# Stages ahead of attention in a one-layer hybrid trunk: six raw weight tiles for four, 36- and 64-row transposes on all 128 rows, another order of the first products and of what stands between them

## The chip, the cores and the metric

One core of a Trainium2 chip runs the kernel. The metric is the device time of one execution in microseconds. All rows named "profile" come from one execution taken by the hardware profiler.

## The reference, cut to what matters

One layer (DEPTH is 1) on 512 tokens of 1024 channels, all in fp32: a norm, one wide projection, a pooling mixer and a sparse-attention mixer side by side, a gated merge, and an MLP.

```python
h = rms_norm(x, norm_mix[l])
proj = h @ w_in[l]
u, q, kc, vc, ksl, vsl, kwn, vwn, g_nsa, g_merge = jnp.split(proj, IN_SPLITS, axis=-1)
y_pool = pool_mixer(u, w_pool[l], pool_scale[l])
y_nsa = nsa_mixer(q, kc, vc, ksl, vsl, kwn, vwn, g_nsa, pe_k[l], pe_v[l],
                  w_ck1[l], w_ck2[l], w_cv1[l], w_cv2[l]).astype(x.dtype)
merged = g_a * (y_pool @ w_proj_pool[l]) + g_b * (y_nsa @ w_proj_nsa[l])
x = x + merged @ w_out[l]
h = rms_norm(x, norm_mlp[l])
x = x + jnp.square(jax.nn.relu(h @ w_ff1[l])) @ w_ff2[l]
```

Inside the attention mixer, blocks of 32 keys and of 32 values are compressed by a small MLP each, which is what most of the stages ahead of attention prepare:

```python
flat = blocks.transpose(0, 1, 3, 2, 4).reshape(B, n_cmp, G, CMP_LEN * dh)
return jax.nn.gelu(flat @ w1) @ w2
```

## The kernel before, in words

**Products in three parts.** A product of fp32 operands is made from split operands: a high part (rounded to the type float32r) and a low part (what is left). Three matmuls follow for each chunk of 128 channels: high by high, low weights by high tokens, high weights by low tokens. In the rows, `wh` and `wl` are the high and low parts of a weight tile; `R_64` and `R_65` (both `R` in the profile) are the high and low parts of the normed, transposed tokens; `wkt` holds both parts of a compression weight.

**Weights.** A weight comes as a raw tile of up to 128 x 1024 fp32 (512 KB) by a DMA that is issued from SyncE's queue (`emit_load`, L297). Raw tiles are taken in turn from a ring of RAW = 4 buffers, so a load waits until the tile four loads earlier has been converted. `emit_prep_half` converts a tile in two halves: the high part by ScalarE (L524; POOL L522 in the very first), the low part by a subtraction on VectorE or, for the first two weights, on POOL (both L527). `ahead()` issues the next piece of this preparation; it is called between groups of products.

**The start.** The four token tiles x0 to x3 are loaded. For each, `sums0` takes the sum of squares (ScalarE L793, L794) and scales the tile (VectorE L796, L799); `turn0` transposes it on TensorE, eight blocks of 128 x 128 (L807); `evac0` takes the blocks out of PSUM into the high part (ScalarE L815) and the low part (VectorE L817). For tiles 2 and 3 `evac0` also copies the blocks to a buffer MA (ScalarE L820), which the gates of the merge use much later. `token_sums` adds high and low parts of the tokens into MA, two such sums early on (VectorE L1142). `fm_halves` (L700) makes the first two products, the compression keys `ck` and the selection keys `ks`, in halves of 256 tokens: first both keys on tiles 0 and 1, then both on tiles 2 and 3. Between them a side generator, `others()`, is stepped: it emits the transposes and evacuations of tiles 2 and 3, after every twelfth product.

**Up to attention.** A list written by hand, P1, sets the order: ck, ks, u0, wk0, u1, wk1, u2, wk2, kw, wk3, cv, V0, V1, V2, wv0, u3, wv1, q0, wv2, the pool products, wv3, gates, the other queries. `cmp_first` takes ck (or cv) from PSUM to a scratch tile with the tokens of each block beside each other (ScalarE L963, L966), adds the position rows (VectorE L973) and splits the result into the operand cA (VectorE L976, L979). `cmp_mlp1` multiplies it by the compression weights wk0 to wk3 or wv0 to wv3 (TensorE L997, eight products of 256 columns each). `cmp_rest` applies the activation, transposes two blocks of 64 rows (L1022), takes them out with a scale (ScalarE L1025) and makes the second compression product (L1035 for keys, L1050 for values). The pooling mixer works on the u tiles (VectorE L1083 to L1095, TensorE psF<-yd,wpl). `rope` turns keys and queries with help of a small DMA `rs<-rx` from SyncE (L882) that exchanges halves.

**From attention on.** Attention takes some 180 to 365 us of the span, the merge and output projection follow, and the MLP runs to the end. Sums of several weight products are prepared in DRAM by accumulating DMAs that POOL issues (L343), in attention too, where POOL also scales the attention rows P (L1423).

TensorE's instructions run in the order in which the program issues them, which a scheduler sets; `behind(x)` (an issue_after) only says that an instruction is placed after x.

Of the kernel before, what the change touches and what calls it, by code (L numbers as in the profile page):

```python
# [62 lines left out]
def trunk(ctx: ExitStack, tc: tile.TileContext, A, out):  # L63
    nc = tc.nc
# [37 lines left out]
    WL, LD = [], []  # L102
    RAW = 4

# [166 lines left out]
    raws, hls = {}, {}  # L271
    st = {"load": 0, "prep": 0, "use": 0, "kept": 0, "pairs": 0, "sums": 0}
    spare, slots_hl = [], []
# [4 lines left out]
    def emit_load():  # L278

        i = st["load"]  # L280
        if i >= len(LD):
            return False
        segs = LD[i]
        a = segs[0][0].shape[1]
        b = sum(s.shape[2] for s, _ in segs)
        assert a * b <= 1024
        if not by_name() or st["kept"] < RAW:
            st["kept"] += by_name()
            t = wp.tile([128, 1024], F32, tag="raw", bufs=RAW, name=f"raw{i}")
        elif spare:  # L290
            t = spare.pop(0)
        else:
            return False
        st["load"] += 1
        v = t[:, :a * b].rearrange("p (a b) -> p a b", a=a)
        for s, o in segs:
            began[0] = nc.sync.dma_start(v[:, :, o:o + s.shape[2]], s)  # L297
        raws[i] = (t, a, b)
        for _ in range(sums_after(i)):
            make_sum(began[0])  # L300
        while i in EARLY[1:] and begun:
            add_sum()
        if (26 <= i < N1 and len(begun) > 1) or i >= N1 + len(FILL2) + 4 and (len(begun) > 2 or begun and st["sums"] == len(jobs)):
            add_sum()
        while i == MLP0 + 6 and len(begun) > 2:
            add_sum()
        return True
# [379 lines left out]
    def fm_halves(keys, psp, posts, tag, xT):  # L687

        ws, ps = [], []
        for h in range(2):  # L690
            tok = slice(256 * h, 256 * h + 256)
            for i, k in enumerate(keys):
                if h == 0:
                    ws.append(use(k))
                    ps.append(psp.tile([128, S], F32, tag=tag[0], bufs=tag[1], name="psF"))
                prods = fm_products(ws[i][0], ws[i][1], xT, tok=tok)
                if h == 0:
                    prods = prods[0::3] + prods[2 - i::3] + prods[1 + i::3]
                for j, (a, b) in enumerate(prods):
                    last_mm[0] = PE.matmul(ps[i][:, tok], a, b, start=h == 0 and j == 0,  # L700
                                           stop=h == 1 and j == len(prods) - 1, skip_group_check=True)
                    if j % 12 == 11:
                        ahead()
                        step_side()
                if h == 1:
                    r = posts[i](ps[i])
                    if r is not None:
                        side.append(r)
                yield
# [31 lines left out]
    PC = ap.tile([128, NT, 2, 64], FR, name="PC")  # L741
    rows = early_f[1][0:36, 0:128]
    w2 = {kv: f[:, 1824:1952].rearrange("p (k c) -> p k c", k=2) for kv, f in zip("vk", early_f)}
# [10 lines left out]
    for h in range(2):  # L754
        for r in (slice(0, 96), slice(96, 127)):
            DVE.memset(grow[r, 512 * h:512 * h + 512], 0.0)
    ACT.dma_start(xt[0], x_d[0:128, :])
    nc.sync.dma_start(xt[1], x_d[128:256, :])
# [27 lines left out]
    def behind(made):  # L786
        return tc.issue_after(made.ins)
# [13 lines left out]

    def turn0(i):
        trs[i] = []
        for a in range(2):
            pt = ps1.tile([128, 4, 128], F32, tag="V", bufs=4, name="psTr")
            for k in range(4):
                PE.transpose(pt[:, k, :], xt[i][:, 512 * a + 128 * k:512 * a + 128 * k + 128], ident)  # L807
            trs[i].append(pt)

    def evac0(i, after=None, root=None):  # L810
        sl = slice(128 * i, 128 * i + 128)
        for a in range(2):
# [3 lines left out]
            with behind(after) if after else nullcontext():  # L816
                v = DVE.tensor_tensor(hT[1][:, ks, sl], trs[i][a], hT[0][:, ks, sl].bitcast(F32), op=ALU.subtract)  # L817
        for a in range(2 if i > 1 else 0):
            c = 128 * (i - 2)
            ACT.activation(quarter(MAf, 2 * a + 1)[:, :, c:c + 128], trs[i][a], AF.Copy)  # L820
        return r, v
# [8 lines left out]
    with behind(r):  # L830
        r, scaled2 = sums0(2)
    mode["first"] = ACT
# [3 lines left out]
    with behind(conv[0]):  # L836
        root3, v = sums0(3)
    mode["first"] = None
# [3 lines left out]
    def others():  # L842

        yield
        for i in (2, 3):
            with behind(last_mm[0]):
                turn0(i)
            made[:] = evac0(i, v, root3)
            yield

# [7 lines left out]
    c0.close()  # L858
    made0 = list(made)
    with behind(made[0]):  # L860
        ACT.activation(tick, rr[3][:, 1:2], AF.Sigmoid)
# [78 lines left out]
    with ExitStack() as c1:  # L940
# [64 lines left out]
        def cmp_rest(kv, ps):  # L1005
            t = early_f[0][0:64, 1056:1824].rearrange("p (a n) -> p a n", a=3)
            z, b, c = t[:, 0], t[:, 1], t[:, 2]
            ACT.activation(b, ps[64:128, :], AF.Copy)
# [9 lines left out]
            for _ in range(14 if kv == "v" else 9):  # L1018
                yield
            pt = ps1.tile([128, 2, 64], F32, tag="M", bufs=2, name="psM")  # L1020
            for i in range(2):
                PE.transpose(pt[:, i, :], b[:, 128 * i:128 * i + 128], ident[0:64, 0:64])  # L1022
            gt = p1.tile([128, 2, 64], F32, tag="cg", bufs=2, name="cg")
            with tc.high_priority(60):
# [7 lines left out]
            if kv == "k":  # L1032
                for e in range(2):
                    for i in range(2):
                        PE.matmul(pm[:, e, :], w2d[:, i, e, :], gt[:, i, :], start=i == 0, stop=i == 1,  # L1035
                                  skip_group_check=True)
# [11 lines left out]
            else:  # L1048
                for i in range(2):
                    PE.matmul(pm[0:64, 0, :], gt[:, i, :], w2["v"][:, i, :], start=i == 0, stop=i == 1,  # L1050
                              skip_group_check=True)
                yield
                for g in range(2):
                    for o in range(2):
# [5 lines left out]
                                           op0=ALU.mult, op1=ALU.mult)  # L1060

        wpl = [p1.tile([128, 4, 128], FR, name=f"wpl{e}") for e in range(2)]
        dest["wpool"] = [w.rearrange("p g c -> p (g c)") for w in wpl] + ["wpool"]
# [70 lines left out]
        def token_sums():  # L1134
# [5 lines left out]
            for b in ("11", "21"):  # L1140
                with behind(made0[1] if b == "21" else scaled2):
                    DVE.tensor_tensor(xq[b], *(v.bitcast(F32) for v in parts[b]), op=ALU.add)  # L1142
                yield
                yield
# [44 lines left out]
        first_posts += [lambda ps: list(cmp_first("k")(ps)).clear(), lambda ps: rope(ps, -0.125, k_done(0))]  # L1189
        pr = ps1.tile([128, 36], F32, tag="M", bufs=2, name="psM")  # L1190
        PE.transpose(pr, rows, ident[0:36, 0:36])
        DVE.tensor_copy(pec, pr)
        for _ in first:
# [891 lines left out]
```

## Time and profile before

| what | value |
|---|---|
| median of 3 runs | 770.54 us (770.27 to 772.26) |
| span of the profiled execution | 767.4 us |
| what lies around the span, median less span | 3.1 us |
| TensorE busy | 756.7 us (99%) |
| VectorE busy | 666.4 us (87%) |
| ScalarE busy | 511.1 us (67%) |
| POOL busy | 184.2 us (24%) |
| granted TensorE clock | full speed in every slice |

The page gives no time of its own for the profiled execution, only its span; the median of the runs is 3.1 us longer. In the timeline a row is a group of instructions of one kind: its start, its busy time, engine, line, operation, output and inputs, and in brackets how long the engine was idle ahead of it and what it waited for. Matmuls overlap, and their ends are modelled, so a group's cost is best read from its start to the start of the next group.

### The profile page before, as it was taken

Reading aid. Unit: us, or ns where it says so; the run is one execution under the profiler, and the core shown is the slowest. Engines: PE = TensorE matmul, PEld = TensorE weight load, DVE = VectorE, ACT = ScalarE, POOL = GpSimd, SP = SyncE. Lnnn points to the kernel's source line nnn. Section 1 sums busy time; section 2 is a strip of 40 time slices with the busy share of each in tenths; the row PEclk is TensorE's granted clock in tenths of the full one; section 3 lists DMA queues with packets and bytes.
Section 4 is the critical chain, followed back from the end, with each engine's and each line's share of the span. In section 5 each row is a group of like instructions: output and inputs, shape, how many; then the busy total and the mean of one; then the engine's idle time right before and its main releaser. Section 6 shows DMA issues by size and latency. Waiting matters only on the chain.

```text
span 767.4 us, 13409 instructions
## 1 busy us (share of the span) xinstructions
PE 756.7 (99%) x4757; PEld 675.9 (88%) x4757; DVE 666.4 (87%) x1279; ACT 511.1 (67%) x977; POOL 184.2 (24%) x264
## 2 busy tenths in 40 slices
PE   9999999999999999999999999999999999999996
PEld 7889889888888888888889899989998999889985
DVE  7897999548988889989689689997989788978897
ACT  7766655328878888898745576954774477447754
POOL 4001010117746766574000200111111110111001
PEclk9999999999999999999999999999999999999999
DMA  9559993983051833371357965989998999799942
GB/s 308 165 143 266 251 230 108 257 214 115 15 176 52 158 56 70 56 138 60 116 186 220 324 111 185 287 219 299 310 259 222 314 303 257 215 325 294 293 171 110
DMA packets 119886, 150.76 MB, mean 196 GB/s; under 512 B 5782, under 2 KB 92346, under 8 KB 119611
## 3 DMA queue, kind: packets, MB, share of 16 engines
q1 hardware_dynamic: 98250, 122.90, 48.3%
q0 software_dynamic: 21280, 26.22, 22.8%
q8 instruction: 38, 0.62, 0.3%
q10 hardware_dynamic: 288, 0.79, 0.3%
q14 instruction: 30, 0.24, 0.1%
HBM read 145.16 MB, written 54.53 MB: 260 GB/s over the span
## 4 chain that ended last, share of the span: by engine, by line
PE 84%; DVE 9%; ACT 2%; DMA 2%; issue 1%; POOL 1%; SPq 0%; DVEq 0%; ACTq 0%; POOLq 0%
PE psB L638 20%; PE psB L1698 18%; PE psF L568 16%; PE psB L568 6%; PE psV L638 5%; PE psS L1378 4%; PE psT L1440 4%; PE psO L1474 4%; PE psB L1647 3%; DMA raw<-w_in 2%; PE psF L700 1%; DVE wl L527 1%; DVE PT L1456 1%; DVE P L1400 1%; DVE wkt L527 1%
## 5 line engine op out<-in xcount | busy, mean ns | idle before, releaser
L343 POOL DMA_DIRECT2D S<-w_ff x44 | 49.0, 1113 | 351.3 <-DMA S<-w_ff 290.3
L568 PE MATMUL psF<-R,wh 128*128 128x512 f32 x384 | 124.6, 400 | 0.0
L390 ACT ACTIVATE wh<-raw 128x1024 fp32r<-128x1024 f32 x73 | 77.1, 1058 | 70.0 <-PE psB L638 24.0
L1423 POOL TENSOR_SCALAR P<-P,sm,GT 128x128 f32<-128x128 f32 (+3 forms) x128 | 85.5, 724 | 68.8 <-DVE sm L1420 36.1
L395 DVE TENSOR_TENSOR wl<-raw,wh 128x1024 fp32r<-128x1024 f32 x73 | 88.9, 1219 | 12.7 <-ACT wh L390 12.2
L568 PEld LDWEIGHTS psF<-R,wh 128*128 128x128 f32 x384 | 68.8, 188 | 11.4 <-issue 0.2
L1410 ACT ACTIVATE P<-P,sm 128x128 f32<-128x128 f32 (+3 forms) x128 | 71.0, 557 | 9.9 <-DVE sm L1400 6.2
L568 PE MATMUL psF<-R,wl 128*128 128x512 f32 x192 | 75.5, 393 | 0.0
L524 ACT ACTIVATE wh<-raw 128x512 fp32r<-128x512 f32 (+1 forms) x76 | 45.1, 616 | 32.9 <-PE psF L568 21.2
L1400 DVE CUSTOM_DVE_ANT_0 P<-psS,cst 128x128 f32<-128x128 f32 (+3 forms) x128 | 59.3, 482 | 4.9 <-PE psT L1440 2.7
L390 ACT ACTIVATE w3h<-raw 128x1024 fp32r<-128x1024 f32 x37 | 39.2, 1059 | 34.0 <-PE psB L638 12.6
L527 DVE TENSOR_TENSOR wl<-raw,wh 128x512 fp32r<-128x512 f32 (+1 forms) x74 | 51.5, 707 | 9.2 <-ACT wh L524 8.9
L1451 ACT ACTIVATE PT<-psT 128x512 fp32r<-128x512 f32 (+2 forms) x96 | 49.0, 520 | 13.9 <-PE psT L1440 13.0
L1456 DVE TENSOR_TENSOR PT<-psT,PT 128x512 fp32r<-128x512 f32 (+2 forms) x96 | 56.2, 591 | 1.5 <-ACT PT L1451 1.3
L1440 PE MATMUL psT<-ident,P 128*128 128x128 f32 x320 | 50.1, 273 | 0.6 <-POOL rx L899 0.4
L395 DVE TENSOR_TENSOR w3l<-raw,w3h 128x1024 fp32r<-128x1024 f32 x37 | 45.1, 1220 | 4.7 <-ACT w3h L390 4.5
L1474 PE MATMUL psO<-PT,VV 128*128 128x256 f32 x320 | 48.5, 286 | 0.0
L1440 PEld LDWEIGHTS psT<-ident,P 128*128 128x128 f32 x320 | 39.6, 140 | 9.4 <-POOL rx L899 0.8
L638 PE MATMUL psB<-R,wh 128*128 128x256 f32 x336 | 46.3, 279 | 0.0
L1474 PEld LDWEIGHTS psO<-PT,VV 128*128 128x128 f32 x320 | 42.2, 188 | 1.3 <-ACT PT L1451 0.3
L638 PEld LDWEIGHTS psB<-R,wh 128*128 128x128 f32 x336 | 42.5, 188 | 0.2
L568 PEld LDWEIGHTS psF<-R,wl 128*128 128x128 f32 x192 | 36.0, 188 | 7.5
(442 smaller groups left out, 2083.7 us busy)
## 6 DMA issues: line engine op xcount, KB each, us to landing
raw<-w_ff SPq DMA_DIRECT2D x54, 512.0 KB, 6.2
S<-w_ff POOLq DMA_DIRECT2D x44, 512.0 KB, 8.2
raw<-S SPq DMA_DIRECT2D x44, 512.0 KB, 5.3
S<-w_ff SPq DMA_DIRECT2D x32, 512.0 KB, 7.3
raw<-w_in SPq DMA_DIRECT2D x31, 512.0 KB, 4.7
S<-S SPq DMA_DIRECT2D x12, 512.0 KB, 6.7
raw<-w_proj_nsa SPq DMA_DIRECT2D x8, 512.0 KB, 4.1
x<-x SPq DMA_DIRECT2D x7, 512.0 KB, 6.5
```

Of the source, the lines that this page charges most:

```text
L390: ACT.activation(h, t, AF.Copy)
L395: DVE.tensor_tensor(l, t, h.bitcast(F32), op=ALU.subtract)
L527: eng.tensor_tensor(l[:, sl], t[:, sl], h[:, sl].bitcast(F32), op=ALU.subtract)
L568: PE.matmul(ps, a, b, start=first and j == 0, stop=last and j == n - 1, skip_group_check=True)
L638: PE.matmul(out, w[u][:, k, 128 * f:128 * f + 128], moving[v][:, k, :], **kw)
L1400: DVE.tensor_tensor_reduce(out=P[:, o:o + n].rearrange("p (a c) -> p a c", c=128), in0=s, in1=m, scale=1.0, scalar=3e38, op0=ALU.add, op1= ...
L1410: last_exp[:] = [ACT.activation(c, c, AF.Exp, bias=sm[:, 0, e:e + 1], scale=-1.0, accum_out=sm[:, 1, e:e + 1])]
L1423: r = POOL.tensor_scalar(P[:, o:o + n], P[:, o:o + n], sm[:, 2, e:e + 1], GT[:, qb, c + e:c + e + 1], op0=ALU.mult, op1=ALU.mult)
L1440: PE.transpose(pt[:, 128 * j:128 * j + 128], P[:, 128 * j:128 * j + 128], ident)
L1456: return DVE.tensor_tensor(dL, src, dH.bitcast(F32), op=ALU.subtract)
L1474: PE.matmul(ps[:, qb % 2, :, :], VV[:, k, b, g, :], t[:, j, :, :], start=False, stop=last and j == len(kbs) - 1 and t is tL, skip_group_ch ...
L1698: PE.matmul(ps[f], self.Y.of(y)[u][:, 2 * g + k, 128 * f:128 * f + 128], w[v][:, k, :], start=first and g == k == u == v == 0, stop=g == k ...
```

## The change

1. **Six raw tiles.** RAW goes from 4 to 6. Each raw tile takes 4 KB of every partition; the 8 KB come from the scratch space for the descriptors of POOL's DMAs, which goes from the default of 16384 to 8192 bytes. Two loads more are issued behind the first products, and at load N1 (where attention's loads begin) two calls of `emit_load` do nothing, so that from there on the loads are again four tiles ahead until the MLP.
2. **First products.** In the first half, ck goes high by high, low tokens, low weights (before: low weights second). ks keeps its order.
3. **Tiles 2 and 3.** Their transposes come one half (four blocks) at a time, after products 30, 32, 40 and 44 of the 48, for all eight blocks of a tile in two steps.
4. **Copies and sums.** The four copies to MA come after the last evacuation, and the first token sum comes there too, before behind the scaling of tile 2.
5. **Padding.** The transpose of the 36 rows of positions and scales works on 128 rows (one more memset of 128 x 128 on VectorE at the start), the two transposes in `cmp_rest` work on 128 rows in place of 64 (one more memset of 64 x 256 on POOL), with an output of 128 x 256; L1050's product goes to all 128 rows. The buffer `cg` goes from two copies to one.

```diff
-    RAW = 4
+    RAW = 6
...
+        if i == N1 and st["spared"] < 2:
+            st["spared"] += 1
+            return True
...
                 if h == 0:
-                    prods = prods[0::3] + prods[2 - i::3] + prods[1 + i::3]
+                    prods = prods[0::3] + prods[1::3] + prods[2::3]
...
                     if j % 12 == 11:
                         ahead()
+                    if j % 12 == 11 if h else 24 * i + j + 1 in (30, 32, 40, 44):
                         step_side()
...
-    rows = early_f[1][0:36, 0:128]
+    rows = early_f[1][:, 0:128]
...
+    DVE.memset(rows, 0.0)
...
-        for a in range(2 if i > 1 else 0):
-            c = 128 * (i - 2)
-            ACT.activation(quarter(MAf, 2 * a + 1)[:, :, c:c + 128], trs[i][a], AF.Copy)
...
     def others():
-        yield
         for i in (2, 3):
-            with behind(last_mm[0]):
-                turn0(i)
-            made[:] = evac0(i, v, root3)
-            yield
+            for a in range(2):
+                with behind(last_mm[0]):
+                    turn0(i, (a,))
+                if a:
+                    made[:] = evac0(i, scaled3, root3)
+                yield
+        for i in (2, 3):
+            for a in range(2):
+                c = 128 * (i - 2)
+                with behind(made[0]):
+                    ACT.activation(quarter(MAf, 2 * a + 1)[:, :, c:c + 128], trs[i][a], AF.Copy)
...
+    with behind(made[0]):
+        for _ in range(2):
+            emit_load()
...
-            t = early_f[0][0:64, 1056:1824].rearrange("p (a n) -> p a n", a=3)
-            z, b, c = t[:, 0], t[:, 1], t[:, 2]
+            t = early_f[0][:, 1056:1824].rearrange("p (a n) -> p a n", a=3)
+            turn = t[:, 1]
+            z, b, c = (t[0:64, i] for i in range(3))
...
-            pt = ps1.tile([128, 2, 64], F32, tag="M", bufs=2, name="psM")
+            pt = ps1.tile([128, 2, 128], F32, tag="M", bufs=2, name="psM")
             for i in range(2):
-                PE.transpose(pt[:, i, :], b[:, 128 * i:128 * i + 128], ident[0:64, 0:64])
-            gt = p1.tile([128, 2, 64], F32, tag="cg", bufs=2, name="cg")
+                PE.transpose(pt[:, i, :], turn[:, 128 * i:128 * i + 128], ident)
+            gt = p1.tile([128, 2, 128], F32, tag="cg", bufs=1, name="cg")
...
-                    PE.matmul(pm[0:64, 0, :], gt[:, i, :], w2["v"][:, i, :], start=i == 0, stop=i == 1,
+                    PE.matmul(pm[:, 0, :], gt[:, i, :], w2["v"][:, i, :], start=i == 0, stop=i == 1,
...
+        POOL.memset(early_f[0][64:128, 1312:1568], 0.0)
...
-                with behind(made0[1] if b == "21" else scaled2):
+                with behind(made0[1]):
                     DVE.tensor_tensor(xq[b], *(v.bitcast(F32) for v in parts[b]), op=ALU.add)
...
-        PE.transpose(pr, rows, ident[0:36, 0:36])
-        DVE.tensor_copy(pec, pr)
+        PE.transpose(pr, rows, ident)
+        DVE.tensor_copy(pec, pr[:, 0:36])
...
-    nc = bacc.Bacc("TRN2", target_bir_lowering=False, num_devices=1)
+    nc = bacc.Bacc("TRN2", target_bir_lowering=False, num_devices=1, dynamic_dma_scratch_size=8192)
```

The order on TensorE, first halves of ck and ks, before (a name's number tells one buffer from another: wh_216 and wl_217 are ck's weight, wh_258 and wl_259 ks's, x_157 and x_158 token tiles 2 and 3):

```order
L700 MATMUL psF<-R_64,wh_216 128x256 x8
L700 MATMUL psF<-R_64,wl_217 128x256 x8
L700 MATMUL psF<-R_65,wh_216 128x256 x8
L807 MATMUL psTr<-ident,x_157 128x128 x4
L700 MATMUL psF<-R_64,wh_258 128x256 x2
L807 MATMUL psTr<-ident,x_157 128x128 x4
L700 MATMUL psF<-R_64,wh_258 128x256 x6
L700 MATMUL psF<-R_65,wh_258 128x256 x7
L807 MATMUL psTr<-ident,x_158 128x128 x4
L700 MATMUL psF<-R_65,wh_258 128x256
L700 MATMUL psF<-R_64,wl_259 128x256
L807 MATMUL psTr<-ident,x_158 128x128 x4
```

And the same place now (wh_217 and wl_218 are ck's weight, wh_259 and wl_260 ks's):

```order
L703 MATMUL psF<-R_64,wh_217 128x256 x8
L703 MATMUL psF<-R_65,wh_217 128x256 x8
L703 MATMUL psF<-R_64,wl_218 128x256 x8
L703 MATMUL psF<-R_64,wh_259 128x256 x6
L812 MATMUL psTr<-ident,x_157 128x128 x4
L703 MATMUL psF<-R_64,wh_259 128x256 x2
L812 MATMUL psTr<-ident,x_157 128x128 x4
L703 MATMUL psF<-R_65,wh_259 128x256 x8
L812 MATMUL psTr<-ident,x_158 128x128 x4
L703 MATMUL psF<-R_64,wl_260 128x256 x4
L812 MATMUL psTr<-ident,x_158 128x128 x4
L703 MATMUL psF<-R_64,wl_260 128x256 x4
```

ck's products with the low weights now stand third, tile 2's transposes stand six products further back, and tile 3's last transposes stand three products further back than before.

On VectorE, from the scaling of tile 2 to the copy of the position rows, before:

```order
L796 RECIPROCAL r_202<-r_202 128x1
L799 SCALAR_TENSOR_TENSOR x_157<-x_157,r_202,psM 128x512 x2
L1142 TENSOR_TENSOR MA<-R_64,R_65 128x1024
L796 RECIPROCAL r_203<-r_203 128x1
L799 SCALAR_TENSOR_TENSOR x_158<-x_158,r_203,psM 128x512 x2
L817 TENSOR_TENSOR R_65<-psTr,R_64 128x4x128 x4
L857 CAST identR<-ident 128x128
L1142 TENSOR_TENSOR MA<-R_64,R_65 128x1024
L1192 COPY pec<-psM 128x36
```

And now:

```order
L801 RECIPROCAL r_203<-r_203 128x1
L804 SCALAR_TENSOR_TENSOR x_157<-x_157,r_203,psM 128x512 x2
L801 RECIPROCAL r_204<-r_204 128x1
L804 SCALAR_TENSOR_TENSOR x_158<-x_158,r_204,psM 128x512 x2
L822 TENSOR_TENSOR R_65<-psTr,R_64 128x4x128 x4
L865 CAST identR<-ident 128x128
L1155 TENSOR_TENSOR MA<-R_64,R_65 128x1024 x2
L1205 COPY pec<-psM 128x36
```

The first token sum has gone from between the scalings of tiles 2 and 3 to behind the low parts of both.

On SyncE's queue, the loads of the fifth raw tile and on, before (raw4 is the fifth):

```order
L297 DMA raw4_222<-w_in 128x8x128
L297 DMA raw5_264<-w_ck1 128x4x256
L297 DMA raw6_360<-w_in 128x8x128
L297 DMA raw7_419<-w_ck1 128x4x256
L882 DMA rs_468<-rx_467 32x512 x4
L297 DMA raw8_482<-w_in 128x8x128
L297 DMA raw9_512<-w_ck1 128x4x256
```

And now:

```order
L300 DMA raw4_223<-w_in 128x8x128
L300 DMA raw5_265<-w_ck1 128x4x256
L300 DMA raw6_357<-w_in 128x8x128
L300 DMA raw7_365<-w_ck1 128x4x256
L300 DMA raw8_367<-w_in 128x8x128
L300 DMA raw9_425<-w_ck1 128x4x256
L893 DMA rs_474<-rx_473 32x512 x4
```

Two loads more stand ahead of the first exchange of halves, and each load waits for the tile six loads earlier in place of four. Further on, in attention, one accumulating DMA of POOL stands two stretches earlier and another later than before.

More of the change, by code (lines that the diff above doesn't have):

```diff
@@ L271, in trunk @@
     raws, hls = {}, {}
-    st = {"load": 0, "prep": 0, "use": 0, "kept": 0, "pairs": 0, "sums": 0}
+    st = {"load": 0, "prep": 0, "use": 0, "kept": 0, "pairs": 0, "sums": 0, "spared": 0}
     spare, slots_hl = [], []
@@ L800, in sums0, with turn0 @@
         return r, v
-    def turn0(i):
-        trs[i] = []
-        for a in range(2):
+    def turn0(i, halves=range(2)):
+        trs.setdefault(i, [])
+        for a in halves:
             pt = ps1.tile([128, 4, 128], F32, tag="V", bufs=4, name="psTr")
@@ L830, in trunk @@
     with behind(r):
-        r, scaled2 = sums0(2)
+        r, _ = sums0(2)
     mode["first"] = ACT
@@ L836, in trunk @@
     with behind(conv[0]):
-        root3, v = sums0(3)
+        root3, scaled3 = sums0(3)
     mode["first"] = None
@@ L1034, in cmp_rest @@
                     for i in range(2):
-                        PE.matmul(pm[:, e, :], w2d[:, i, e, :], gt[:, i, :], start=i == 0, stop=i == 1,
+                        PE.matmul(pm[:, e, :], w2d[:, i, e, :], gt[:, i, 0:64], start=i == 0, stop=i == 1,
                                   skip_group_check=True)
@@ L1189, in trunk @@
         first_posts += [lambda ps: list(cmp_first("k")(ps)).clear(), lambda ps: rope(ps, -0.125, k_done(0))]
-        pr = ps1.tile([128, 36], F32, tag="M", bufs=2, name="psM")
-        PE.transpose(pr, rows, ident[0:36, 0:36])
-        DVE.tensor_copy(pec, pr)
+        pr = ps1.tile([128, 128], F32, tag="M", bufs=2, name="psM")
+        PE.transpose(pr, rows, ident)
+        DVE.tensor_copy(pec, pr[:, 0:36])
         for _ in first:
```

## The prediction

> **What bounds the kernel now.** I read the page first, then busy time by stretches, then the timeline of each engine where TensorE waits. The page:
>
> ```profile
> span 767.4 us, 13409 instructions
> ...
> PE 756.7 (99%) x4757; PEld 675.9 (88%) x4757; DVE 666.4 (87%) x1279; ACT 511.1 (67%) x977; POOL 184.2 (24%) x264
> ```
>
> TensorE is busy for 99% of the span. An edit can only gain where TensorE waits or where its own instructions take less. Busy time by stretches (columns: length, then each engine's busy time):
>
> ```profile
> 60.00:80.00 20.00, 20.00 (x125) 18.31 (x124) 15.47 (x33) 14.05 (x30) 3.55 (x3) 1.00 1.07 261
> 80.00:100.00 20.00, 19.30 (x139) 17.95 (x138) 19.28 (x34) 13.10 (x21) 2.01 (x2) 1.00 0.97 243
> ...
> 240.00:300.00 60.00, 59.61 (x391) 52.95 (x391) 54.47 (x188) 50.63 (x141) 38.32 (x60) 1.00 0.52 107
> ...
> 420.00:760.00 340.00, 340.00 (x2189) 309.51 (x2189) 302.34 (x380) 211.10 (x303) 36.56 (x33) 1.00 0.88 250
> ```
>
> Ahead of attention one stretch (80 to 100) has a wait of TensorE, after one in which VectorE had 4.5 of 20 us free. In the MLP TensorE is busy for 340.00 of 340 us: six raw tiles can shorten nothing there, and I cost them at nothing. TensorE itself hides this, and the cover would have to shrink by more than any wait there shows.
>
> **First products: ck's low tokens ahead of its low weights.** TensorE's timeline:
>
> ```profile
> 10.81 0.63 PE L700 MATMUL psF<-R,wl 128*128 128x256 f32 x4
> 11.78 0.74 PE L700 MATMUL psF<-R,wl 128*128 128x256 f32 x4 [0.34 <-POOL wl L527]
> 12.36 1.11 PE L700 MATMUL psF<-R,wh 128*128 128x256 f32 x8
> 13.31 0.60 PE L807 MATMUL psTr<-ident,x 128*128 128x128 f32 x4
> 13.66 0.48 PE L700 MATMUL psF<-R,wh 128*128 128x256 f32 x2
> 13.98 0.60 PE L807 MATMUL psTr<-ident,x 128*128 128x128 f32 x4
> ...
> 16.62 0.60 PE L807 MATMUL psTr<-ident,x 128*128 128x128 f32 x4
> ...
> 17.96 0.25 PE L1191 MATMUL psM<-ident,ea 36*128 36x36 f32 x1
> ```
>
> Eight products without a wait take 13.31 - 12.36 = 0.95 us, 0.119 each. The eight with low weights take 12.36 - 10.81 = 1.55, so 0.60 goes to waiting for POOL. POOL, VectorE and ScalarE at the same place:
>
> ```profile
> 9.19 2.53 POOL L527 TENSOR_TENSOR wl<-raw,wh 128x512 fp32r<-128x512 f32 x2
> ...
> 12.43 3.54 POOL L527 TENSOR_TENSOR wl<-raw,wh 128x512 fp32r<-128x512 f32 x2
> 8.68 2.48 DVE L817 TENSOR_TENSOR R<-psTr,R 128x512 fp32r<-128x512 f32 x4
> ...
> 13.03 1.77 DVE L1142 TENSOR_TENSOR MA<-R,R 128x1024 f32<-128x1024 f32 x1
> 16.58 1.27 ACT L815 ACTIVATE R<-psTr 128x512 fp32r<-128x512 f32 x2 [1.36 <-PE psTr L807]
> ```
>
> The low tokens are done at 8.68 + 2.48 = 11.16, with all but the last quarter before 10.81; they run 10.81 to 11.76, and the low weights (ready at 9.19 + 2.53 = 11.72) follow at once, to 12.71. ck ends 0.60 earlier. ks and its 16 transposes then last 17.96 - 13.31 = 4.65 as before: 24 x 0.119 = 2.86, and 16 x 0.11 (13.66 - 13.31 is 0.35 for four, with the step to the next product) = 1.76, together 4.62. Its low weights are ready at 12.43 + 3.54 = 15.97 and used, second half, after 20 products and 16 transposes, at 12.71 + 4.14 = 16.85: the new POOL memset ahead of them has 0.88 us of room. If that cover goes, each 0.1 us over it costs 0.1. Tile 3's scaling, freed of the sum at 13.03, is ready before its transposes.
>
> This 0.60 does not all reach the end. The last transposes now start at 12.71 + 24 x 0.119 - 4 x 0.119 + 12 x 0.11 = 16.41 in place of 16.62: only 0.21 earlier, and from them hangs the chain to the first compression product:
>
> ```profile
> 21.88 0.69 DVE L527 TENSOR_TENSOR wkt<-raw,wkt 128x512 fp32r<-128x512 f32 x1 [1.65 <-ACT wkt L524]
> ...
> 28.51 1.28 DVE L979 TENSOR_TENSOR cA<-scratch,cA 128x512 fp32r<-128x512 f32 x2
> 29.34 1.16 PE L997 MATMUL psC<-wkt,cA 128*128 128x256 f32 x8
> ```
>
> ScalarE does the same work after the evacuation as before, in another order, and so is 0.21 earlier. The first half of cA is ready at 28.51 + 0.64 = 29.15, 0.19 ahead of TensorE; now at 28.94. TensorE would come at 28.74 and waits to 28.94 or a little over. **I take 0.35 here**, between 0.21 and 0.60. The token sum that moved took 1.77 us beside POOL; behind the split it lies in the 1.65 us in which VectorE waited before 21.88. The 0.12 over that would only make wkt's low parts late, and they have until 29.34.
>
> **Padding.** Around the 64-row transposes:
>
> ```profile
> 65.80 0.30 PE L568 MATMUL psV<-wh,R 128*128 128x304 f32 x1
> 66.03 0.33 PE L1022 MATMUL psM<-ident,ea 64*128 64x64 f32 x2
> ...
> 66.53 0.30 PE L568 MATMUL psV<-wl,R 128*128 128x304 f32 x1
> 66.67 0.44 PE L568 MATMUL psV<-wh,R 128*128 128x304 f32 x2
> ```
>
> From 65.80 to 66.53 lie two products and two transposes, 0.73 us. Products alone take 66.67 - 66.53 = 0.14. At 128 rows, four transposes and two products take 13.98 - 13.31 = 0.67, of which 0.44 are the four at 0.11; the step into and out of them costs nothing that shows. So the padded pair takes 2 x 0.14 + 2 x 0.11 = 0.50: 0.23 less, twice (keys, values), 0.46. L1050 goes from 64 columns to 128 and loses one such step in and out; I estimate 0.1, the step in alone. The 36-row transpose at 17.96 takes no more than it did, ahead of a place where TensorE waits; nothing. **Together 0.55.** The trace has no padded transpose between products of this shape, so the bounds are 0.7 (L1050 saves as much as a pair) and -0.44 (each of four costs 0.11 more).
>
> The low end has a rule behind it. The Trainium skill, TensorEngine Tiling (Array Packing), "When to Use Tiling", recommends two row tiles where the contraction is 64, and by that padding to 128 rows gives away half the array; the sum by it would be the -0.44. The rows above speak against it here, since nothing runs in the other half.
>
> **Loads two tiles further ahead.** The wait of TensorE in 80 to 100 and what it hangs from (the second last row is from the chain that ended last):
>
> ```profile
> 87.03 0.96 PE L997 MATMUL psC<-wkt,cA 128*128 128x256 f32 x6
> 88.69 0.50 PE L997 MATMUL psC<-wkt,cA 128*128 128x256 f32 x2 [0.70 <-DVE wkt L527]
> 75.69 0.76 DVE L527 TENSOR_TENSOR wpl<-raw,wpl 128x256 fp32r<-128x256 f32 x2 [2.02 <-ACT wpl L524]
> ...
> 87.95 0.68 DVE L527 TENSOR_TENSOR wkt<-raw,wkt 128x512 fp32r<-128x512 f32 x1
> 72.90 5.29 DMA raw<-w_in
> 79.26 0.58 ACT L1077 ACTIVATE ea<-psF 128x512 f32<-128x512 f32 x1
> ```
>
> Six products from 87.03 end at 87.03 + 6 x 0.119 = 87.74; the next starts at 88.69 behind wv3's low part (87.95 + 0.68 = 88.63): 0.95 lost. VectorE is late because it had been idle for 2.02 before 75.69, behind a load, and because the load at 72.90 could not start until a raw tile came free. With six tiles both start two conversions earlier. What VectorE could take up at once is limited by u3's tokens, out of TensorE at 79.26 + 0.58 = 79.84, where it is at other conversions until 81.14: 1.30 to be made up. So wv3's low part comes at 88.63 - 1.30 = 87.33, less 0.58 where TensorE's own gain ahead (0.35 + 0.23) is passed on to u3: 86.75. TensorE would be there at 87.74 - 0.58 = 87.16. **The wait goes, 0.95**; if the gain is not passed on, 0.2 of it stays. What is late next is the gate operand at 89.03, with a margin that I cannot read better than some tenths.
>
> SyncE's queue: the exchange of halves of ks now stands behind two loads more.
>
> ```profile
> 24.40 0.39 SPq L297 DMA_DIRECT2D raw<-w_ck  x1
> 27.02 2.51 SPq L882 DMA_DIRECT2D rs<-rx  x4
> ```
>
> The two loads ahead of it wait, now as before, for the third and the fourth raw tile, and leave at the same times, the second at 24.40; the exchange still waits for its data, to 27.02. Nothing.
>
> **Sum.** 0.35 + 0.55 + 0.95 = 1.85, about 1.9. The profiled span would be 765.5; the median stands 3.1 above the span (770.54 - 767.4), which gives **768.6**. TensorE's saturation behind 108 us carries the gain to the end, but attention's order of POOL's sums shifts, which I allow half a us either way.
>
> **Rivals.** *More comes through.* Attention has waits too:
>
> ```profile
> 194.15 0.50 PE L1378 MATMUL psS<-KH,Q 128*128 128x512 f32 x1 [0.36 <-DVE sm L1400]
> ...
> 227.24 0.47 PE L1378 MATMUL psS<-KH,Q 128*128 128x512 f32 x1 [0.45 <-DVE sm L1400]
> ```
>
> If the whole 0.60 of the head passes (+0.25) and an altered order closes both waits (0.81), the gain is 1.9 + 1.0 = 2.9: 767.6. For it: the chain at 29.34 is tight by 0.2 only. Against: nothing in the change touches the softmax behind these waits.
>
> *The middle stays.* If VectorE's run before wv3 follows other work than loads, the wait at 88.69 takes in the 0.58 that was gained ahead of it, and only what lies behind is left, 0.23 + 0.1 = 0.33 at the least; if u3's tokens pass the 0.58 on to VectorE as well, 0.33 + 0.58 = 0.91. That is 769.6 to 770.2, say 769.9. For it: VectorE is busy for 19.28 of 20 us there. Against: the 4.5 us free just before. That the six tiles do not do what they say, since tiles come free as late as before, comes to the same.
>
> *Slower: half the descriptor space.* POOL issues accumulating sums in attention among the scalings of P that TensorE waits for:
>
> ```profile
> 245.63 1.17 POOL L343 DMA_DIRECT2D S<-w_ff  x1
> ...
> 250.21 1.14 POOL L343 DMA_DIRECT2D S<-w_ff  x1
> ...
> 253.48 1.27 POOL L343 DMA_DIRECT2D S<-w_ff  x1
> S<-w_ff POOLq DMA_DIRECT2D x44, 512.0 KB, 8.2
> ```
>
> A sum lands 8.2 us after its issue. If half the space holds one sum and not two, the issue at 250.21 has to wait to 253.83, and the third to some 262: 3.6 and 8.5 us in which POOL scales nothing. POOL is free for 21.7 of 60 us in 240 to 300, so perhaps 5 of the 12 reach TensorE: 768.6 + 5 = 773.6. It decides from two sums outstanding that do not fit. For it: these three are that close. Against: each issue takes 1.2 us with up to two outstanding, with no sign of a full ring. The Trainium skill, Debugging Trainium Hangs, "Descriptor Overflow", names too many descriptors for the scratch (16 KiB a partition) on the Pool queue as a cause of a hang; no run here shows where that point lies.
>
> **How the numbers follow.** Chances: forecast 0.46 (own range 768.0 to 769.3), more comes through 0.25, the middle stays 0.22, slower 0.07. A measurement of this kernel tells 0.3%, 2.3 us, from no change: faster is below 768.2, slower above 772.9. A third of the forecast's cases and four fifths of the first rival's are faster: 0.15 + 0.20 = 0.35. Slower is the last rival, 0.07; the rest, 0.58, is within. The range goes from the first rival's far end (the step out of L1050 saved too) to beyond the second's: 766.9 to 770.8.
>
> **What would show it.** Right: no gap at the low weights of ck, and ks's transpose of position rows some 0.6 us earlier; the first compression product 0.3 to 0.4 earlier with a short wait for cA; from the product before L1022 to the second product behind it 0.50; no wait before wv3's last products; VectorE's free time in 60 to 80 below 4.5 us; attention starting 1.9 us earlier. Wrong: a wait of the same size at wv3, POOL's issues at L343 well over 1.2 us, or attention's own length changed by more than 0.5 us.

## The result and the profile after

The changed kernel took 774.76 us (median of 6 runs, 774.05 to 778.26), the kernel before 770.4 (769.57 to 772.26). The ratio is 1.0064 [1.0047, 1.0081]: slower by 0.6%, and outside the predicted range. The profiled execution took 775.91 with a span of 774.1, so 1.8 us lie around the span. The same 1.8 stands in every later profiled run, so the profiled execution of before took about 769.2, 1.2 less than that kernel's median; the prediction's 3.1 was too much.

The page of after:

```profile
span 774.1 us, 13406 instructions
...
PE 758.6 (98%) x4757; PEld 677.1 (87%) x4757; DVE 667.3 (86%) x1280; ACT 510.7 (66%) x977; POOL 184.3 (24%) x265
```

TensorE's idle time is 774.1 - 758.6 = 15.5 us, before it was 767.4 - 756.7 = 10.7. Its busy time has grown by 1.9 as well, with the same 4757 products. To find the place I set each product's start against that of the same product before. After minus before is +0.77 at the first products, -0.02 at 25 us, +0.5 from 30 to 60, -0.5 behind 88, -1.0 from 120 to 240, -0.5 from 244 to 360, +0.04 at 378, +2.0 at 396, and +6.7 from 430 to the end. So ahead of attention the change gained 0.77 + 1.02 = 1.79 against its own start, where 1.85 was forecast. 0.5 went at 243, and 7.2 between 360 and 430, where the prediction looked at nothing. The same in busy time by stretches, after (length, then each engine's busy time, the granted clock, the DMA share, GB/s):

```profile
80.00:100.00 20.00, 20.00 (x143) 18.81 (x142) 19.13 (x34) 13.74 (x20) 2.33 (x2) 1.00 0.95 251
...
240.00:300.00 60.00, 59.65 (x390) 52.79 (x390) 54.52 (x187) 49.86 (x139) 38.03 (x60) 1.00 0.41 80
...
360.00:385.00 25.00, 24.37 (x119) 19.50 (x117) 14.63 (x28) 15.90 (x29) 3.86 (x4) 1.00 0.98 252
...
410.00:415.00 5.00, 2.08 (x14) 1.67 (x14) 5.00 (x8) 3.00 (x5) 0.00 (x0) 0.97 1.02 173
415.00:420.00 5.00, 5.00 (x33) 5.00 (x32) 4.55 (x7) 3.43 (x4) 0.00 (x0) 0.68 0.77 250
```

And before, two of these stretches:

```profile
360.00:385.00 25.00, 25.00 (x126) 21.15 (x125) 17.13 (x32) 17.69 (x32) 1.10 (x1) 1.00 0.45 147
...
410.00:415.00 5.00, 5.00 (x45) 5.00 (x44) 5.00 (x7) 5.00 (x8) 1.18 (x1) 1.00 0.45 152
```

The wait at wv3 is gone (20.00 of 20 us, before 19.30). Between 360 and 385 the DMA share has gone from 0.45 to 0.98, and from 380 on TensorE waits. Its waits there in after:

```profile
385.08 0.50 PE L571 MATMUL psB<-R,wl 128*128 128x512 f32 x1 [0.68 <-DVE wl L530]
396.73 0.50 PE L571 MATMUL psB<-R,wl 128*128 128x512 f32 x1 [0.47 <-DVE wl L530]
410.67 0.38 PE L1660 MATMUL psB<-wh,R 128*128 128x256 f32 x1 [0.33 <-ACT wh L474]
413.65 0.39 PE L1660 MATMUL psB<-wl,R 128*128 128x256 f32 x1 [2.60 <-DVE wl L477]
...
415.73 0.42 PE L1660 MATMUL psB<-wh,R 128*128 128x256 f32 x1
415.94 0.41 PE L1660 MATMUL psB<-wl,R 128*128 128x256 f32 x1
```

All four wait for a weight's conversion: 0.68 + 0.47 + 0.33 + 2.60 = 4.1. The last two rows show why busy time grew: 415.94 - 415.73 = 0.21 from product to product, where 0.12 is the usual step. The granted clock is 0.68 in that stretch, and over the 3.5 us from 414.6 to 418.1 this costs about 1.5. Together 5.6 of the 7.2. Counted from start to start, with the slower steps around each wait, the four waits take 5.4. A loss of 0.55 at 372, which the first experiment has too, comes on top, and some 0.2 is regained behind 420.

What filled the DMA queues is on SyncE's own queue. Before (start, length, line, what is moved):

```profile
373.54 0.38 SPq L297 DMA_DIRECT2D raw<-w_out  x1
...
429.77 0.52 SPq L335 DMA_DIRECT2D S<-S  x1
430.33 1.25 SPq L335 DMA_DIRECT2D S<-w_ff  x2
431.68 0.56 SPq L335 DMA_DIRECT2D S<-S  x1
```

And after:

```profile
361.25 0.50 SPq L338 DMA_DIRECT2D S<-S  x1
...
362.42 1.34 SPq L338 DMA_DIRECT2D S<-w_ff  x2
373.55 0.39 SPq L300 DMA_DIRECT2D raw<-w_out  x1
...
415.28 0.51 SPq L338 DMA_DIRECT2D S<-S  x1
```

Four sums of the MLP's weights (each a copy of 512 KB by SyncE, then an accumulating DMA by POOL) began at 430 to 432. Now three of them leave at 361 to 364 and the fourth at 415. The output weights that attention's end needs leave at the same time as before, 373.55, behind the three. How long each load is under way in 360 to 385 (KB each, median us to landing), before:

```profile
raw<-w_out SPq DMA_DIRECT2D x3, 512.0 KB, 3.7
```

and after, with the sums beside it, and ScalarE's conversion of the weight that left at 373.55:

```profile
S<-w_ff POOLq DMA_DIRECT2D x3, 512.0 KB, 8.6
...
raw<-w_out SPq DMA_DIRECT2D x2, 512.0 KB, 8.9
...
382.47 0.63 ACT L527 ACTIVATE W1H<-raw 128x512 fp32r<-128x512 f32 x1 [6.47 <-DMA raw<-w_out]
```

3.7 became 8.9, and ScalarE stood 6.47 us waiting for it.

Why the sums left there is in the code. They are tied to the number of a load, not to a time: `sums_after` makes four with load `MLP0 + 6`, and `emit_load` adds those that are still begun at the same number. Loads from `MLP0` on, the first of the MLP, take the ring's tiles as long as `kept < RAW`: six of them now, before it was four. The next one needs a tile that another stage hands back. So the tile that attention hands back at about 360 (L1612) receives load `MLP0 + 6`, and the four sums with it, where before it received `MLP0 + 4`. The order in which the program issues SyncE's instructions already shows it: the copies of the first three sums stand some twenty rows further up.

### The profile page after: what moved, and what is told of

Its sections match the earlier page's. It is cut to its first block, busy times and chain, and to the rows that moved or that the text cites. A ratio compares the mean times of both kernels' runs of the same rounds, so it can differ in the third digit from the quotient of the medians.

```text
span 774.1 us, 13406 instructions
## 1 busy us (share of the span) xinstructions
PE 758.6 (98%) x4757; PEld 677.1 (87%) x4757; DVE 667.3 (86%) x1280; ACT 510.7 (66%) x977; POOL 184.3 (24%) x265
## 4 chain that ended last, share of the span: by engine, by line
PE 83%; DVE 9%; ACT 4%; DMA 2%; issue 1%; POOL 0%; DVEq 0%; ACTq 0%; POOLq 0%; SPq 0%
PE psB L641 20%; PE psB L1711 18%; PE psF L571 17%; PE psV L641 5%; PE psB L571 4%; PE psS L1391 4%; PE psT L1453 4%; PE psO L1487 3%; PE psB L1660 2%; PE psV L571 2%; PE psF L703 1%; DVE P L1413 1%; DMA raw<-w_out 1%; DVE PT L1469 1%; PE psC L1008 1%
```

## The experiments

The theory: the four sums at load `MLP0 + 6` cost nearly all of the loss, and what was gained ahead of attention is still there without them. Rivals: the halved descriptor space; the new head or the padding, by what they bring later; the two further tiles themselves.

**The sums put back, in the changed kernel.**

```diff
-        while i == MLP0 + 6 and len(begun) > 2:
+        while i == MLP0 + 8 and len(begun) > 2:
-            return {3: 1, 6: 4}.get(i - MLP0, 0)
+            return {3: 1, 8: 4}.get(i - MLP0, 0)
```

> The changed kernel with one edit: the four sums that were tied to the seventh MLP load (index 6) are tied to the ninth (index 8), so they leave SyncE's queue where they stood before the change. Theory 1 (these sums, issued at 361 us, take the DMA from the output weights): the waits of TensorE at 384, 396 and 410 and the lower clock behind the last one go, about 6 us of the span; what is gained ahead of attention stays. TensorE stood 0.5 us earlier than before at 360, with a start that was 0.8 late, so 770.4 - 1.3 = 769.1, between 768.4 and 769.9. Theory 2 (half the descriptor space slows POOL's sums): no change, 774 to 775. Theory 3 (loads that run further ahead delay the output weights by themselves): no change, 774 to 775.

Measured: 769.91 (11 runs) against 769.79, ratio 0.9999 [0.999, 1.0008]. The sums leave at 427 again, as before the change:

```profile
426.76 0.52 SPq L338 DMA_DIRECT2D S<-S  x1
```

The loss is gone, and the output weights' loads take 4.1 in place of 8.9, so the sums are its cause. But no gain is left, where 769.1 was expected. Product by product it stands at -1.21 from 120 to 240, then loses 0.34 at 243, 0.55 at 372 and 0.5 at 414. At the first two something still comes earlier than before: a sum of POOL's stands two stretches further up in attention, and the conversion of W1H comes ahead of other work on ScalarE at 372. At 414 TensorE waits shortly for R.

**The sums moved up, in the kernel before.**

```diff
-        while i == MLP0 + 6 and len(begun) > 2:
+        while i == MLP0 + 4 and len(begun) > 2:
-            return {3: 1, 6: 4}.get(i - MLP0, 0)
+            return {3: 1, 4: 4}.get(i - MLP0, 0)
```

> The kernel before with one edit: the same four sums are tied to the fifth MLP load (index 4) and not the seventh, which is the load that goes to the spare tile behind attention. Nothing else of the change is in it: four raw tiles, the full descriptor space, the old order of the head. Theory 1: the sums leave at about 361 us, the output weights land late, TensorE waits between 380 and 415 and the clock falls behind the longest wait: 4 to 7 us more, 774 to 777. Theories 2 and 3: 770.4, no change.

Measured: 777.55 (5 runs) against 769.79, ratio 1.0102 [1.0085, 1.012]. Its TensorE:

```profile
386.65 0.73 PE L568 MATMUL psB<-R,wh 128*128 128x512 f32 x2 [0.81 <-ACT wh L524]
```

Nothing of the change is in this kernel, and moving the sums alone makes the loss, with the first wait at the same place. By the medians it is larger here (7.8 against 4.2 below). In the profiles the loss behind 360 is nearly the same: 6.1 here against before, 6.2 in after against the first experiment. Of the rest, 1.8 lies here between 88 and 114 us, ahead of the sums, and after's profiled execution was 1.2 above its median. The loss is not made up alike: the granted clock stays at 1.00 here, though a fall was expected, and 2.6 are lost at products that run between 439 and 462 in before, where after loses nothing. Why they are lost there is open.

**Everything but the six tiles.** The changed kernel with four raw tiles, without the two loads more and with the whole descriptor space.

```diff
-    RAW = 6
+    RAW = 4
...
-        for _ in range(2):
-            emit_load()
-    with behind(made[0]):
...
-    nc = bacc.Bacc("TRN2", target_bir_lowering=False, num_devices=1, dynamic_dma_scratch_size=8192)
+    nc = bacc.Bacc("TRN2", target_bir_lowering=False, num_devices=1)
```

> The changed kernel without its first part: four raw tiles, no two extra loads, the full descriptor space; the order of the first products, the transposes, the copies and the padding stay. Theory 1: the sums stand where they stood before, so no loss; the head gives 0.2 to 0.35, the padding 0.55, the wait before wv3's last products (0.95) stays: 769.5 to 769.8. A rival, that parts 2 to 5 shift attention or the MLP by themselves, gives 771 or more.

Measured: 770.24 (11 runs), ratio 1.0003 [0.9993, 1.0013]. Head and padding together gain nothing that can be measured. The wait at wv3 is there, and one behind it that the profile of before did not have:

```profile
89.41 0.50 PE L1002 MATMUL psC<-wkt,cA 128*128 128x256 f32 x2 [0.70 <-DVE wkt L527]
...
94.16 3.42 PE L638 MATMUL psV<-TS,wkt 128*128 128x256 f32 x24 [0.72 <-ACT wkt L428]
```

**Half the descriptor space alone, in the kernel before.**

```diff
-    nc = bacc.Bacc("TRN2", target_bir_lowering=False, num_devices=1)
+    nc = bacc.Bacc("TRN2", target_bir_lowering=False, num_devices=1, dynamic_dma_scratch_size=8192)
```

> The kernel before with half the descriptor space for POOL's DMAs and nothing else. Theory 1 and theory 3: 770.4, and each issue of a sum by POOL takes the 1.1 us that it takes before. Theory 2 and the slower rival of the prediction: the issues that follow each other within 8 us wait for room, 772 or more, with issues well over 1.2 us.

Measured: 769.79 (10 runs), ratio 0.9998 [0.9986, 1.001]. The three issues that the prediction's slower rival was built on:

```profile
246.60 1.17 POOL L343 DMA_DIRECT2D S<-w_ff  x1
...
251.15 1.14 POOL L343 DMA_DIRECT2D S<-w_ff  x1
...
254.42 1.27 POOL L343 DMA_DIRECT2D S<-w_ff  x1
```

1.17, 1.14 and 1.27, to the digit as before. The rival is refuted: half the space holds what is outstanding here.

**Six tiles only until attention.** The changed kernel, but the two further tiles serve only loads ahead of `N1`; from attention on, four tiles and the order of before.

```diff
-    RAW = 6
+    RAW = 4
...
-            t = wp.tile([128, 1024], F32, tag="raw", bufs=RAW, name=f"raw{i}")
+            two = i < N1 and i % 6 > 3
+            t = wp.tile([128, 1024], F32, tag="rawx" if two else "raw", bufs=2 if two else RAW, name=f"raw{i}")
```

> The changed kernel, in which the two extra raw tiles are two buffers of their own, used for two loads of every six up to attention and by none behind it; from there on four tiles in turn, as before the change, and the sums tied to the same loads as before. On ScalarE, VectorE, POOL and SyncE the order from attention to the end is then that of before. Theory 1, widened: what the first experiment lost behind 240 us (0.34 at 243, 0.55 at 372, 0.5 at 414) came from loads and sums that leave earlier because a tile is free earlier. Then none of the three is left, TensorE arrives at the end as early as it leaves 120 us: 1.2 to 1.7 before the profiled run of before, and 2 or more before its median: 767.5 to 768.5. Rival: the three losses are answers to TensorE being earlier, and come again: 769.5 to 770.

Measured: 768.38 (8 runs) against 770.01, ratio 0.9971 [0.9957, 0.9984]. What stands ahead of 240 us now reaches the end: -0.55 at 120, -0.61 at the end against a start of +0.49. So the three later losses of the first experiment, too, belong to what the two further tiles do from attention's loads on. One new wait has come:

```profile
69.88 1.08 PE L1048 MATMUL psM<-cg,w2d 128*128 128x64 f32 x8 [0.78 <-ACT cg L1038]
```

**The two tiles alone, in the kernel before.** The edit above, the two loads more, the two loads spared at `N1` and half the space; the head and the transposes are those of before.

```diff
+        if i == N1 and st["spared"] < 2:
+            st["spared"] += 1
+            return True
...
+            two = i < N1 and i % 6 > 3
+            t = wp.tile([128, 1024], F32, tag="rawx" if two else "raw", bufs=2 if two else RAW, name=f"raw{i}")
...
+        for _ in range(2):
+            emit_load()
+    with behind(made[0]):
```

> The kernel before, with only the two buffers of the fifth experiment and the two loads more (the old head, no padding). By the prediction it takes away the wait before wv3's last products, 0.95. The three other profiles of the old weights' ring show 0.5 to 2 us lost between 86 and 114 us, more than the profile of before; if that comes from loads, TensorE goes through this stretch without it in this kernel: 768.5 to 769.2. Rival: the stretch is bound by VectorE's own work: 769.8.

Measured: 768.1 (5 runs) against 770.01, ratio 0.9965 [0.9952, 0.9979]. Once more on another chip:

> The kernel before with the two buffers until attention and the two loads more, once more, beside the ninth experiment on the same chip: 768.1 again, with no wait of TensorE at the compression weights near 88 us and none for POOL's low weights near 11 us if the first token tile lands as late as in seven of the eight profiles so far.

Measured: 768.13 (8 runs) against 770.2, ratio 0.9976 [0.9965, 0.9987]. So the two tiles alone are at least as fast as with all the rest, and faster than both kernels. Its TensorE:

```profile
10.10 1.37 PE L704 MATMUL psF<-R,wh 128*128 128x256 f32 x8
11.30 1.10 PE L704 MATMUL psF<-R,wl 128*128 128x256 f32 x8
12.23 1.10 PE L704 MATMUL psF<-R,wh 128*128 128x256 f32 x8
...
29.36 1.16 PE L1004 MATMUL psC<-wkt,cA 128*128 128x256 f32 x8
...
87.02 1.10 PE L1004 MATMUL psC<-wkt,cA 128*128 128x256 f32 x8
```

This is the old head, in the first of the two profiles, and it has no wait at ck's low weights. All eight products at wv3 run in one piece.

**Without the padding, and with the copies moved.** Three more, each on the kernel with two tiles until attention. The first takes the padding back: 64 and 36 rows as before, with the copy cg at 64 columns. Its central line:

```diff
-                PE.transpose(pt[:, i, :], turn[:, 128 * i:128 * i + 128], ident)
+                PE.transpose(pt[:, i, :], b[:, 128 * i:128 * i + 128], ident[0:64, 0:64])
```

> The fifth experiment's kernel without the padding of the transposes (36 and 64 rows again, 64 columns at the values' second product). By the prediction the padding gives 0.55: this kernel is then slower by that than the fifth, with 0.73 and not 0.50 between the products around each transpose pair. By the changed kernel's trace the keys' pair gives 0.24 and loses 0.24 two microseconds later, where the second compression product waits for the copy: then only 0.3 to 0.35.

Measured: 768.46 (9 runs), ratio 0.9974 [0.9964, 0.9985], as with the padding. The products behind cg have no wait:

```profile
68.78 0.28 ACT L1036 ACTIVATE cg<-psM 128x128 f32<-128x128 f32 x1
...
69.19 0.30 PE L572 MATMUL psV<-wh,R 128*128 128x304 f32 x1
69.33 1.00 PE L1046 MATMUL psM<-cg,w2d 128*128 128x64 f32 x8
```

The second moves ScalarE's four copies into MA from the head to behind the keys' loop (removed here, and put in unchanged there):

```diff
-        for i in (2, 3):
-            for a in range(2):
-                c = 128 * (i - 2)
-                with behind(made[0]):
-                    ACT.activation(quarter(MAf, 2 * a + 1)[:, :, c:c + 128], trs[i][a], AF.Copy)
```

> The fifth experiment's kernel with the four copies to MA behind the compression keys' posts in the program: three of them go on ScalarE behind the copies to scratch, so the chain to the first compression product has three copies less, 1.5 us. The changed kernel waits there for 0.56 at 29 us. Theory: the wait goes, and the kernel is faster by 0.5 than the fifth: 767 to 768. Rival: the copies now delay the next weights on ScalarE, and the wait comes back at u0 or wk1.

Measured: 768.21 (12 runs), ratio 0.9976 [0.9964, 0.9987]. The wait for cA is gone, but the time isn't distinguishably better:

```profile
10.64 2.19 PE L704 MATMUL psF<-R,wh 128*128 128x256 f32 x16 [0.44 <-ACT R L821]
...
29.44 1.10 PE L1004 MATMUL psC<-wkt,cA 128*128 128x256 f32 x8
```

The third does both:

> The two buffers until attention, the new order of the head, the four copies to MA behind the compression keys' posts, no padding. From the first product to the first compression product the old head takes 19.26 to 19.28 us where TensorE does not wait for POOL's low weights, the new head 19.51 to 19.53 with a wait for cA, and the new head with the copies moved 18.80. Theory: 18.8 here too, no wait for the copy cg at 69 us, since that belongs to the padding; together 0.4 to 0.5 better than the kernel before with two tiles, 767.3 to 767.8 beside its 768.1. Rival: the copies behind the posts hold up the next weights on ScalarE, and it is no better: 768.1 to 768.5.

Measured: 768.4 (9 runs) against 770.2, ratio 0.9976 [0.9966, 0.9985]. That is what the rival expected: no version that keeps the new head has a median below that of the two tiles alone. The 18.8 us that were expected did not come either:

```profile
10.26 2.35 PE L704 MATMUL psF<-R,wh 128*128 128x256 f32 x16
...
29.46 1.10 PE L1003 MATMUL psC<-wkt,cA 128*128 128x256 f32 x8
```

29.46 - 10.26 = 19.20. And the products behind cg wait again (69.12 - 68.79 = 0.33 where 0.14 is a step), though there is no padding here.

The whole, as differences to each kernel's own runs of before:

| step | from | us |
| --- | --- | --- |
| two tiles until attention | 768.1 - 770.01 (again: 768.13 - 770.2) | -1.9 (-2.1) |
| head and padding added | -1.63 less -1.91 | +0.3 |
| loads and sums earlier from attention on, without the four | +0.12 less -1.63 | +1.75 |
| the four sums two loads earlier | +4.36 less +0.12 | +4.2 |
| the change | 774.76 - 770.4 | +4.4 |

Each step has an interval of 1 to 1.5 us on either side, so the 0.3 is not to be told from nothing.

## Why the prediction was wrong, step by step

**The step that failed** is "six raw tiles can shorten nothing there, and I cost them at nothing", with its reason, "TensorE itself hides this". That TensorE is busy for 340 of 340 us, from 420 to 760, says that it waits for nothing in the order of before. It says nothing of an order in which the transfers leave elsewhere. The six tiles reach the MLP's loads through `kept < RAW`, and the sums follow the number of the load: in place of nothing this cost 7.2 us in the profile, nearly all of it ahead of that stretch, at weights of the output projection (8.9 us under way in place of 3.7). The prediction saw only POOL's sums in attention shift and allowed "half a us either way"; that place cost 0.5 in after, with a wait that before doesn't have:

```profile
242.61 1.19 PE L1487 MATMUL psO<-PT,VV 128*128 128x256 f32 x8
243.99 0.50 PE L1391 MATMUL psS<-KH,Q 128*128 128x512 f32 x1 [0.20 <-DVE sm L1413]
```

From one start to the next 1.38, before 244.56 - 243.54 = 1.02, and the step behind it is 0.10 longer too. All the rest of the loss lies behind it. None of the rivals had it: the slower one had the right kind of cause, POOL's sums, and the wrong resource, and it was refuted.

**The sum ahead of attention: near, in part by luck.** Of the 1.79 that came where 1.85 was forecast, the head gave 0.22 against that one profile (forecast 0.35), the keys' transposes nothing (0.23), wv3 1.06 (0.95), the values' transposes with L1050 0.34 (0.33), and 0.15 came behind 110 us, where nothing was forecast.

**wv3's wait: right.** 0.95 was forecast. Product by product the stretch around 88 us gained 1.06 in after and 1.07 with the two tiles alone, and VectorE's free time from 60 to 80 fell from 4.5 to 2.4 us in after, as foreseen. The tiles are worth about 2 in all. The profile of before understated them: its execution was 1.2 under its kernel's median, and other profiles with four tiles lose more between 88 and 114, where none with six tiles loses anything. With the sums moved up in the kernel before, 1.8 goes there; one of the waits:

```profile
113.72 1.55 PE L638 MATMUL psV<-TS,wkt 128*128 128x256 f32 x11 [0.21 <-DVE TS L1167]
```

Which load decides in that stretch stays open.

**The head: wrong in sign.** The 0.60 at ck's low weights was there in one execution only. There the first product ran at 9.60. In the four other profiles with the old head it ran at 10.04 to 10.54, since the tokens had landed later (ScalarE took up the first tile at 4.50 to 4.62, there at 4.07), and POOL was done in time. From the first product to the first compression product the old head takes 19.26 to 19.28 in those four, the new one 19.52 in after:

```profile
10.36 2.36 PE L703 MATMUL psF<-R,wh 128*128 128x256 f32 x16
12.56 1.10 PE L703 MATMUL psF<-R,wl 128*128 128x256 f32 x8
...
29.88 1.18 PE L1008 MATMUL psC<-wkt,cA 128*128 128x256 f32 x8 [0.40 <-DVE cA L990]
```

So it is 0.24 slower, by the short wait for cA that the prediction saw as what clips the gain. With the copies into MA moved away that wait goes: 29.44 - 10.64 = 18.80. Not all of that is the wait: without padding, with the copies moved too, it was 19.20. There the stretch with the 36-row transpose takes 0.27 longer (18.26 - 12.45 = 5.81 in place of 18.20 - 12.66 = 5.54), so that this transpose, whose padding the prediction put at nothing, does cost where nothing waits behind it. The first sixteen products take 0.17 longer. In the time of the kernel neither shows.

**Padding: the price was right, and the keys' part is given back.** In after:

```profile
66.32 0.30 PE L571 MATMUL psV<-wh,R 128*128 128x304 f32 x1
...
66.82 0.30 PE L571 MATMUL psV<-wl,R 128*128 128x304 f32 x1
...
69.04 0.30 PE L571 MATMUL psV<-wh,R 128*128 128x304 f32 x1
69.36 1.08 PE L1047 MATMUL psM<-cg,w2d 128*128 128x64 f32 x8
```

66.82 - 66.32 = 0.50, as worked out, where the 64-row pair took 0.73. But the next user of the pair comes 69.36 - 69.04 = 0.32 behind the last product, where 0.14 is a product's step (69.33 - 69.19 without padding): it waits for ScalarE's copy.

```profile
68.56 0.39 ACT L1129 ACTIVATE VV<-psV 128x256 fp32r<-128x256 f32 x1
68.84 0.38 ACT L1037 ACTIVATE cg<-psM 128x256 f32<-128x256 f32 x1
```

It has twice the columns and takes 0.38 in place of 0.28, and a copy of VV now goes ahead of it, which without padding comes behind it. In the kernel with two tiles and the new head that wait is 0.78. How long it is hangs on when ScalarE gets there, and not on the padding alone: with parts 2 to 5 there is none (69.20 - 69.06 = 0.14), and the kernel without padding and with the copies moved has one. The prediction priced the transposes and left out the copy behind them. The values' pair, with L1050, keeps its gain: from the low weights ahead of it to the first product of TS it takes 108.88 - 104.82 = 4.06, before 109.79 - 105.37 = 4.42. On the rule of the Trainium skill, TensorEngine Tiling (Array Packing), "When to Use Tiling", by which two row tiles are to be preferred at a contraction of 64: the padded pair was the cheaper one here, 0.50 against 0.73, with nothing to run in the other half.

## What to carry to other kernels

If loads, sums or other background transfers are placed by an index, a change in the number of buffers moves them all. Compare the order of the DMA queue over the whole program, also where the bounding engine is fully busy, for that busy share holds only as long as its data arrive in time. And before a wait of half a us is made a term of the sum, look whether it exists in a second profile.

## What the runs showed of the hardware

Behind a wait of 2.60 us (2.98 from the product at 410.67 to the one at 413.65) the granted clock is 0.68 from 415 to 420 us, with products 0.21 apart in place of 0.12 for about 3.5 us. So the wait cost half as much again. In the other profiles TensorE waited for at most 0.83 us at a time between 10 us and the last product, and none shows such a fall. The Trainium skill, TensorE: Matmul & The Clock Gate, "HAM oscillation — how this bites in real kernels", gives about 3.4 us as the idle gap to stay under; here no single gap was longer than 2.60. But a wait of 0.33 stands ahead of it with one product between, so TensorE did almost nothing for 3.3 us, and whether 2.60 alone would do is not shown.

A lower granted clock did not always cost time: in the profile without padding and with the copies moved it is 0.95 from 10 us on to the end of the products, yet eight products take 0.93 (12.45 to 13.38), as with a clock of 1.00 where only the copies are moved (12.66 to 13.60, 0.94).

Loads of 512 KB took 8.9 us from issue to landing beside the sums, 3.7 without them in the kernel before, and 4.1 with the sums put back.

The first product started at 9.60 us in one profile and at 10.04 to 10.64 in the others. In the one, ScalarE took up the first token tile at 4.07, in the others at 4.50 to 4.83, and of the five profiles with the old head only that one waits for POOL.
